# Reciprocal roots of the norms: one GpSimd power against eight VectorE steps

## The chip, the cores and the metric

The kernel runs on one core of a Trainium2 chip. The metric is the device time of one execution in microseconds (us), the median of several runs. A core has a matmul engine (PE, with its weight loads shown apart as PEld), a vector engine (DVE), a scalar engine (ACT), GpSimd (POOL) and a sync engine (SP) that issues most transfers. Each engine takes its instructions in the order in which the program lists them for that engine, and waits at an instruction whose inputs are not there yet.

## The reference

Two layers of a decoder trunk run for 256 prompt tokens and 8 sample tokens. Every norm is a root-mean-square norm:

```python
def rmsnorm(x, g):
    xf = x.astype(jnp.float32)
    y = xf * lax.rsqrt(jnp.mean(xf * xf, axis=-1, keepdims=True) + RMS_EPS)
    return (y * g.astype(jnp.float32)).astype(x.dtype)

yp = yp + 0.5 * swiglu(rmsnorm(yp, norm_ffn1[l]), ...)
h = rmsnorm(yp, norm_mix[l])                 # mixer: short convolution beside attention
q = (rmsnorm(q_c, q_a_norm) @ w_q_b)         # low-rank queries
ckv = rmsnorm(kv_c, kv_a_norm)               # low-rank keys and values
merged = concat([rmsnorm(conv_y, gn_conv), rmsnorm(attn_o, gn_attn)])
yp = yp + merged @ w_o
yp = yp + 0.5 * swiglu(rmsnorm(yp, norm_ffn2[l]), ...)
y = rmsnorm(yp, final_norm)                  # at the end
```

## The kernel before

**Layout.** Features lie on the 128 partitions and the 264 tokens (256 and 8) along the free axis. Weights come in chunks of up to 1 MB through three `raw` buffers. A unit of weights is split into a rounded half `hi` (ACT, L230) and a remainder `lo` (DVE, L232), two instructions of each kind per unit; a product is three matmuls, hi by hi, hi by lo, lo by hi (`mm3`, L249 to L251). Five `hi` and five `lo` buffers let units be split ahead of their use. When both units of a chunk are split, the next chunk is loaded.

**A norm.** The squares of a token are summed over the tiles into `ssA` or `ssB`. `sums` reduces 32 x 32 blocks on DVE (L310) and folds them with a small matmul (L311), so that each token's mean stands in one of nine block columns, a tile of 128 x 9. A small DVE instruction adds the epsilon (L345, L562, L909, L933), `rsqrt_of` raises the tile to the power -0.5 on GpSimd (L303), and `over_rows` turns the result into a row that every partition holds (L315). There are thirteen calls of `rsqrt_of`: six from `norm_stats` (each FFN and each mixer), two from `low_rank` (18 columns, keys and queries together), two each from `a_stats` and `c_stats`, and one of 3 columns at the end.

**Order.** The program is traced in an order written by hand (`ORDER` for the mixer; `H1`, `H2`, `N1`, `N2` for the places among the matmuls at which `norm_stats` and `norm_spread` are traced), and a planner then lists each engine's instructions. `behind()` adds an edge: the `lo` instructions that are traced after `after[0]` was set stand behind that instruction on DVE. Buffers of one tag are handed out in the order of tracing: `t264` has nine, `w` has four in the mixer.

**In the mixer** `low_rank` finds the roots for keys and queries, and `latent` spreads those of the keys (`Rk`, a `t264` tile, L315), makes the normalised keys `ckvf` (L570), and takes the query factors (L575, L580). `store_kpe` has matmuls that read `ckvf` (L746), `values` follows (L598 to L600). At the end of the mixer `a_stats` and `c_stats` lead to `a_spread` (L938, L939, `Ra`, L315, L944), whose output the last matmuls of the output projection need.

The tiles that the change touches:

```python
Rk = t264()
over_rows(Rk, s2[:, 0:NBLK])
V.tensor_tensor(ckvf, kvg, Rk[:, :T], ALU.mult)
...
Ra = t264()
over_rows(Ra, fa)
```

Of the kernel before, what the change touches and what calls it, by code (L numbers as in the profile page):

```python
# [7 lines left out]
F32 = mybir.dt.float32  # L8
F32R = mybir.dt.float32r
BF16 = mybir.dt.bfloat16  # L10
I32 = mybir.dt.int32
AF = mybir.ActivationFunctionType
ALU = mybir.AluOpType
AX = mybir.AxisListType
PSUM = bass.MemoryType.PSUM

P = 128
# [3 lines left out]
T = SEQ + NB  # L21

NBLK = -(-T // 32)
TP = 32 * NBLK
# [83 lines left out]
def trunk_kernel(ctx: ExitStack, tc: tile.TileContext, a: dict, o: dict):  # L108
    nc = tc.nc
    V, S, G, PE = nc.vector, nc.scalar, nc.gpsimd, nc.tensor  # L110

    cst = ctx.enter_context(tc.tile_pool(name="cst", bufs=1))
    stat = ctx.enter_context(tc.tile_pool(name="stat", bufs=1))
    tiny = ctx.enter_context(tc.tile_pool(name="tiny", bufs=3))
    tmp = ctx.enter_context(tc.tile_pool(name="tmp", bufs=TMP))
# [9 lines left out]
    def nm(s):  # L125
        n_of[0] += 1
        return f"{s}_{n_of[0]}"

    def t264(dt=F32):
        return tmp.tile([P, TP], dt, tag="t264", name=nm("t264"))  # L130

    def bank(tag):
        if tag == "mm":
            return pmm.tile([P, 512], F32, tag="mm", name=nm("mm"))
        return (paux if tag == "s" else pax3).tile([P, 512], F32, tag=tag, name=nm(tag))

    def small(w, dt=F32, tag=None):
        return tiny.tile([P, w], dt, tag=tag or f"sm{w}", name=nm("sm"))
# [8 lines left out]
    after = [None]  # L147

    def behind():

        return tc.issue_after(after[0]) if after[0] else nullcontext()
# [19 lines left out]
    for l in range(DEPTH):  # L171
# [4 lines left out]
        for c in (0, 2):  # L176
            for part in (1, 2, 0):
                f = part * CD + c * P
# [60 lines left out]
    def take():  # L239
        i = state["next"]  # L240
        state["next"] += 1
        return halves[i]
# [23 lines left out]
    nc.sync.dma_start(con, a["con"])  # L266
    load_chunk()
    tri = t264()[:, 0:P]
    nc.gpsimd.dma_start(tri, a["mask"])

# [11 lines left out]
    def gain(name, n, i=0):  # L282
        return gains[:, gat[name] + n + i:gat[name] + n + i + 1]
# [9 lines left out]
    spre = cst.tile([P, DEPTH, CT, NB], F32, name="spre")  # L293


    mhalf = cst.tile([P, 1], F32, name="mhalf")
    G.memset(mhalf, -0.5)
    fold = cst.tile([P, P], F32, name="fold")
    G.tensor_copy(fold.rearrange("p (a b) -> p a b", a=4), con[:, None, C_SUM:C_SUM + 32].to_broadcast([P, 4, 32]))

    def rsqrt_of(v, w):
        r = small(w, tag=f"rsr{w}")
        G.tensor_tensor(r, v, mhalf.to_broadcast([P, w]), ALU.pow)  # L303
        return r

    def sums(ps, ss, c0=0):


        q = small(NBLK, tag="sums")
        after[0] = V.tensor_reduce(q, ss.rearrange("p (c j) -> p c j", j=32), AX.X, ALU.add, apply_transpose=True).ins  # L310
        PE.matmul(ps[:, c0:c0 + NBLK], fold, q, start=True, stop=True)  # L311

    def over_rows(out, r):

        return V.transpose(out, r[:, :, None].to_broadcast([P, NBLK, 32]))  # L315
# [7 lines left out]
    def finish_y(kt, g, split=True, square=True, pool=False, last=False):  # L323
        if split:
            S.activation(xg["h"][:, kt], y[:, kt], AF.Copy, scale=g)  # L325
            V.scalar_tensor_tensor(xg["l"][:, kt], y[:, kt], g, xg["h"][:, kt].bitcast(F32), ALU.mult, ALU.subtract)  # L326
        if not square:
            return
        if kt == 0:
            S.activation(ssA[:, :T], y[:, kt], AF.Square, scale=D ** -0.5)  # L330
        else:
            sq = t264()
            S.activation(sq[:, :T], y[:, kt], AF.Square, scale=D ** -0.5)
            if kt == KT - 1 and last:
                nrm["sq"] = sq
                return
            (G if pool else V).tensor_tensor(ssA[:, :T], ssA[:, :T], sq[:, :T], ALU.add)
# [3 lines left out]
    def norm_stats():  # L341
        ps = bank("x")
        sums(ps, ssA)
        v = small(NBLK, tag="vn")
        V.tensor_scalar(v, ps[:, 0:NBLK], EPS, None, ALU.add)  # L345
        nrm["v"] = v
        nrm["r"] = rsqrt_of(v, NBLK)
# [23 lines left out]
    def ffn(next_gain, final=False, side=None, first=False):  # L371
# [12 lines left out]
        def evac_g(m, ps):  # L384
            g1 = t264()[:, :T]
            V.tensor_tensor(g1, ps[:, :T], Rb, ALU.mult)  # L386
            done()
            th = t264()[:, :T]
            S.activation(th, g1, AF.Tanh, scale=0.5)  # L389
            a1[m] = t264()[:, :T]  # L390
            evac[0] = V.scalar_tensor_tensor(a1[m], th, 1.0, g1, ALU.add, ALU.mult).ins  # L391
# [96 lines left out]
    def mixer(l):  # L488
# [3 lines left out]
        def mt(shape, tag, dt=F32, bufs=None):  # L492
            return mp.tile(shape, dt, tag=tag, name=nm(tag), **({"bufs": bufs} if bufs else {}))

        def r264():
            return mt([P, T], "r264", F32R, 8)

        def wtile(n=384):
            return mt([P, 384], "w", bufs=4)[:, 0:n]
# [57 lines left out]
        def low_rank():  # L557
            ps = bank("x")
            sums(ps, ssB)
            sums(ps, ssA, NBLK)  # L560
            v2 = small(2 * NBLK, tag="v2")
            V.tensor_tensor(v2.rearrange("p (n c) -> p n c", n=2), ps[:, 0:2 * NBLK].rearrange("p (n c) -> p n c", n=2),  # L562
                            ev[:, None, :].to_broadcast([P, 2, NBLK]), ALU.add)
            st["s2"] = rsqrt_of(v2, 2 * NBLK)

        def latent():
            s2 = st["s2"]
            Rk = t264()
            over_rows(Rk, s2[:, 0:NBLK])
            V.tensor_tensor(ckvf, kvg, Rk[:, :T], ALU.mult)  # L570
            ckh, ckl = r264(), r264()
            S.activation(ckh, ckvf, AF.Copy)

            sel = small(8, tag="qsel")
            V.scalar_tensor_tensor(sel.rearrange("p (c b) -> p c b", b=4), s2[:, NBLK:NBLK + 8].rearrange("p (c b) -> p c b", b=4),  # L575
                                   SCALE, con[:, None, C_BLK:C_BLK + 4].to_broadcast([P, 2, 4]), ALU.mult, ALU.mult)
            qsc = small(2, tag="qsc")
            V.tensor_reduce(qsc, sel.rearrange("p (c b) -> p c b", b=4), AX.X, ALU.add)
            sq8 = small(32, tag="sq8")
            after[0] = V.transpose(sq8, s2[:, 2 * NBLK - 1:2 * NBLK].to_broadcast([P, 32])).ins  # L580
            st["qsc"], st["sq8"] = qsc, sq8[:, 0:NB]
            V.tensor_tensor(ckl, ckvf, ckh.bitcast(F32), ALU.subtract)
            st["ckh"], st["ckl"] = ckh, ckl

            kp2 = t264()
            with behind():
                V.stream_shuffle(kp2[64:96, :T], kp1[64:96, :T], SWAP)
            V.tensor_tensor(kp1[64:96, :T], kp1[64:96, :T], cos[64:96], ALU.mult)
            V.tensor_tensor(kp2[64:96, :T], kp2[64:96, :T], sin[64:96], ALU.mult)
            V.tensor_tensor(kpf[64:96], kp1[64:96, :T], kp2[64:96, :T], ALU.add)  # L590
# [108 lines left out]
        def prompt():  # L699
            low_rank()  # L700
            yield
            latent()
            done(2)
            yield
# [199 lines left out]
        def c_stats():  # L904

            ps = bank("x")
            sums(ps, ssB)
            vc = small(NBLK, tag="vc")
            V.tensor_tensor(vc, ps[:, 0:NBLK], ev, ALU.add)  # L909
            st["sc"] = rsqrt_of(vc, NBLK)  # L910
            st["vc"] = vc
# [24 lines left out]
        def a_spread():  # L936
            fa = small(NBLK, tag="fa")
            V.tensor_tensor(fa, st["sa"], st["sc"], ALU.mult)  # L938
            V.tensor_tensor(fa, fa, st["vc"], ALU.mult)  # L939
            Ra = t264()  # L940
            over_rows(Ra, fa)
            for t in range(CT):
                f = t264()[:, :T]
                V.scalar_tensor_tensor(f, st["attn"][:, t], gain("gn_attn", 4 * l, t), Ra[:, :T], ALU.mult, ALU.mult)  # L944
                S.activation(mg[0][:, t], f, AF.Copy)
                V.tensor_tensor(mg[1][:, t], f, mg[0][:, t].bitcast(F32), ALU.subtract)
# [17 lines left out]
        for k in range(KT):  # L964
            for w, ps in zip(us, pss):
                o_part(ps, w, k)
            if k == 2:
                a_spread()
            if k == 5:
                c_spread()  # L970
            if k == 5:
                c_store()
        for m in range(4):
            o_finish(m, pss[m])
        for m in range(4, KT):
            w, ps = take(), bank("mm")
# [81 lines left out]
    v = small(3, tag="vn")  # L1058
# [11 lines left out]
    r = rsqrt_of(v, 3)  # L1070
# [66 lines left out]
```

## Time and profile before

| what | value |
|---|---|
| median of 3 runs | 1051.21 us (1051.0 to 1051.54) |
| the profiled execution, its own time | 1041.29 us |
| its span, first to last instruction | 1039.5 us |
| mean granted TensorE clock | 0.987 |
| busy: PE, DVE, ACT, POOL | 97%, 72%, 52%, 11% of the span |
| the thirteen powers on POOL | 28.0 us together |

Shares of busy time are means over stages with different limits. A wait row says which engine and line sat idle, what released it, the total, the count and the longest.

### The profile page before, as it was taken

To read this page: it belongs to the slowest core of one execution; us is meant where nothing else is said; L and a number is where in the kernel's file an instruction comes from. 1 tells how busy PE (TensorE), PEld (TensorE's weight loads), DVE (VectorE), ACT (ScalarE), POOL (GpSimd) and SP (SyncE) were. 2 spreads that over 40 slices of the span, in tenths; PEclk is the share of its full clock that TensorE was granted. 3 is DMA by queue.
4 is the path that set the end of the run, shared out by engine and by line. 5 is a ranking of instruction groups with operands and counts; after the bars stand their busy time and mean duration, and the time that the engine had idled before them with its cause. 6 is when DMAs were issued, how large, how long until landed. Compare 5 with 4: busy or idle time off the path is not lost.

```text
span 1039.5 us, 21546 instructions
## 1 busy us (share of the span) xinstructions
PE 1006.8 (97%) x8660; PEld 976.3 (94%) x8660; DVE 751.0 (72%) x1656; ACT 538.0 (52%) x1165; POOL 112.9 (11%) x140
## 2 busy tenths in 40 slices
PE   7999999989999999999999999999899999999996
PEld 6999999979788999999999999999778899999996
DVE  7888876669758877756678888566886887777551
ACT  6555545448535655545455555454675555555441
POOL 2111100040322000000011111001322210000000
PEclk9999999989999999999999999999899999999998
DMA  9767755545615655645557676554553356554531
GB/s 300 232 221 234 234 183 193 164 143 159 258 46 162 211 196 167 198 146 193 190 187 254 210 233 222 164 179 151 161 208 142 108 191 215 169 196 157 179 112 43
DMA packets 170772, 189.98 MB, mean 183 GB/s; under 512 B 3936, under 2 KB 163712, under 8 KB 170672
## 3 DMA queue, kind: packets, MB, share of 16 engines
q1 hardware_dynamic: 164048, 167.53, 50.0%
q0 software_dynamic: 5760, 19.42, 5.2%
q10 hardware_dynamic: 864, 1.64, 0.5%
q8 instruction: 68, 1.11, 0.5%
q14 instruction: 32, 0.26, 0.1%
HBM read 187.12 MB, written 1.49 MB: 181 GB/s over the span
## 4 chain that ended last, share of the span: by engine, by line
PE 70%; issue 20%; DVE 7%; ACT 1%; DMA 1%; POOL 1%; POOLq 0%; ACTq 0%; SPq 0%
PE mm L249 22%; PE mm L251 21%; PE mm L250 21%; DVE lo L232 2%; PE x L780 1%; PE s L650 1%; DVE y L955 1%; DVE xg L326 1%; PE x L819 1%; DMA raw<-in_w_ffn_gate_dram 1%; POOL sm L303 1%; PE x L687 1%; ACT hi L230 1%; PE x L674 1%; DVE t L954 1%
## 5 line engine op out<-in xcount | busy, mean ns | idle before, releaser
L230 ACT ACTIVATE hi<-raw 128x512 fp32r<-128x512 f32 (+1 forms) x648 | 365.4, 612 | 357.0 <-PE mm L250 236.2
L232 DVE TENSOR_TENSOR lo<-raw,hi 128x512 fp32r<-128x512 f32 (+1 forms) x648 | 414.6, 673 | 114.1 <-ACT hi L230 103.9
L249 PE MATMUL mm<-xg,hi 128*128 128x264 f32 x1648 | 472.0, 287 | 8.2 <-DVE t L954 3.1
L251 PE MATMUL mm<-xg,lo 128*128 128x264 f32 x1648 | 468.5, 285 | 0.9 <-DVE lo L232 0.9
L250 PE MATMUL mm<-xg,hi 128*128 128x264 f32 x1648 | 468.5, 284 | 0.0
L249 PEld LDWEIGHTS mm<-xg,hi 128*128 128x128 f32 x1648 | 311.8, 189 | 11.7 <-ACT hi L230 7.1
L251 PEld LDWEIGHTS mm<-xg,lo 128*128 128x128 f32 x1648 | 310.2, 188 | 3.1 <-DVE lo L232 1.8
L250 PEld LDWEIGHTS mm<-xg,hi 128*128 128x128 f32 x1648 | 311.9, 189 | 0.8 <-issue 0.8
L249 PE MATMUL mm<-act,hi 128*128 128x264 f32 x704 | 200.4, 285 | 0.0
L251 PE MATMUL mm<-act,lo 128*128 128x264 f32 x704 | 199.7, 284 | 0.0
L250 PE MATMUL mm<-act,hi 128*128 128x264 f32 x704 | 199.2, 283 | 0.0
L249 PEld LDWEIGHTS mm<-act,hi 128*128 128x128 f32 x704 | 132.3, 188 | 0.2 <-ACT t L1025 0.2
L251 PEld LDWEIGHTS mm<-act,lo 128*128 128x128 f32 x704 | 132.5, 188 | 0.0
L250 PEld LDWEIGHTS mm<-act,hi 128*128 128x128 f32 x704 | 132.4, 188 | 0.0
L456 POOL DMA_INDIRECT nat<-in_cache_ckv_dram,idx x32 | 31.9, 996 | 420.3 <-DVE B L480 187.3
L386 DVE TENSOR_TENSOR t<-mm,Rw 128x264 f32<-128x264 f32 x88 | 37.8, 429 | 43.1 <-PE mm L251 42.8
L395 DVE TENSOR_TENSOR t<-mm,t 128x264 f32<-128x264 f32 x88 | 37.5, 428 | 40.9 <-PE mm L251 40.3
L303 POOL TENSOR_TENSOR sm<-sm,mhalf 128x9 f32<-128x9 f32 (+2 forms) x13 | 28.0, 2155 | 244.6 <-DVE sm L1069 190.4
L325 ACT ACTIVATE xg<-y,gains 128x264 fp32r<-128x264 f32 x48 | 24.1, 513 | 30.0 <-DVE y L441 19.1
L398 DVE TENSOR_TENSOR act<-t,act 128x264 fp32r<-128x264 f32 x88 | 37.7, 429 | 0.9 <-ACT act L397 0.8
L391 DVE SCALAR_TENSOR_TENSOR t<-t,t 128x264 f32<-128x264 f32 x88 | 37.7, 428 | 0.2 <-ACT t L389 0.2
L389 ACT ACTIVATE t<-t 128x264 f32<-128x264 f32 x88 | 36.1, 411 | 2.1 <-DVE t L386 2.1
(219 smaller groups left out, 837.2 us busy)
## 6 DMA issues: line engine op xcount, KB each, us to landing
raw<-in_w_ffn_up_dram SPq DMA_DIRECT2D x44, 1024.0 KB, 5.2
raw<-in_w_ffn_gate_dram SPq DMA_DIRECT2D x43, 1024.0 KB, 5.2
raw<-in_w_ffn_down_dram SPq DMA_DIRECT2D x32, 1024.0 KB, 5.4
raw<-in_w_in_dram SPq DMA_DIRECT2D x14, 1024.0 KB, 5.3
raw<-in_w_ffn_down_dram SPq DMA_DIRECT2D x16, 768.0 KB, 4.6
raw<-in_w_o_dram SPq DMA_DIRECT2D x8, 1024.0 KB, 5.4
raw<-in_w_q_dram SPq DMA_DIRECT2D x2, 768.0 KB, 4.3
raw<-in_w_in_dram SPq DMA_DIRECT2D x2, 640.0 KB, 4.3
```

The source lines that it names most:

```text
L230: S.activation(h[:, k, f], raw[:, k, lo:hi][:, :, f], AF.Copy)
L232: V.tensor_tensor(r[:, k, f], raw[:, k, lo:hi][:, :, f], h[:, k, f].bitcast(F32), ALU.subtract)
L249: PE.matmul(ps, wh, xh, start=start, stop=False)
L250: PE.matmul(ps, wh, xl, start=False, stop=False)
L251: return PE.matmul(ps, wl, xh, start=False, stop=stop)
L303: G.tensor_tensor(r, v, mhalf.to_broadcast([P, w]), ALU.pow)
L386: V.tensor_tensor(g1, ps[:, :T], Rb, ALU.mult)
L389: S.activation(th, g1, AF.Tanh, scale=0.5)
L391: evac[0] = V.scalar_tensor_tensor(a1[m], th, 1.0, g1, ALU.add, ALU.mult).ins
L395: V.tensor_tensor(t, ps[:, :T], a1.pop(m), ALU.mult)
L398: evac[0] = V.tensor_tensor(al[:, m], t, ah[:, m].bitcast(F32), ALU.subtract).ins
L456: G.indirect_dma_start(dst, None, src, bass.IndirectOffsetOnAxis(ap=idx[l][:, b:b + 1], axis=0))
```

## The change

`rsqrt_of` no longer uses GpSimd. It takes a first guess from the bits of the number, as an integer (-0.5 times the bits plus a constant), and improves it in two rounds: three instructions and then four, each reading the one before it. That makes eight DVE instructions on the small tile. `after[0]`, behind which later `lo` instructions stand, is now the last of these eight steps and no longer the block reduce in `sums`. `Rk` and `Ra` come from the tag `w` instead of `t264`, whose tiles shrink from 288 to 266 columns, and the constant `mhalf` is gone.

```diff
     def t264(dt=F32):
-        return tmp.tile([P, TP], dt, tag="t264", name=nm("t264"))
+        return tmp.tile([P, T + 2], dt, tag="t264", name=nm("t264"))
...
-    mhalf = cst.tile([P, 1], F32, name="mhalf")
-    G.memset(mhalf, -0.5)
...
     def rsqrt_of(v, w):
+
         r = small(w, tag=f"rsr{w}")
-        G.tensor_tensor(r, v, mhalf.to_broadcast([P, w]), ALU.pow)
+        t = small(w, tag=f"rst{w}")
+        V.tensor_scalar(r.bitcast(I32), v.bitcast(I32), -0.5, float(0x5F3759DF), ALU.mult, ALU.add)
+        V.scalar_tensor_tensor(t, r, -0.1875, r, ALU.mult, ALU.mult)
+        V.tensor_tensor(t, t, v, ALU.mult)
+        V.scalar_tensor_tensor(r, t, 0.5625, r, ALU.add, ALU.mult)
+        V.scalar_tensor_tensor(t, r, -64.0 / 9.0, r, ALU.mult, ALU.mult)
+        V.tensor_tensor(t, t, v, ALU.mult)
+        V.scalar_tensor_tensor(t, t, 10.0 / 3.0, t, ALU.add, ALU.mult)
+        after[0] = V.scalar_tensor_tensor(r, t, 5.0, r, ALU.add, ALU.mult).ins
         return r
...
-        after[0] = V.tensor_reduce(q, ss.rearrange("p (c j) -> p c j", j=32), AX.X, ALU.add, apply_transpose=True).ins
+        V.tensor_reduce(q, ss.rearrange("p (c j) -> p c j", j=32), AX.X, ALU.add, apply_transpose=True)
...
             s2 = st["s2"]
-            Rk = t264()
+            Rk = wtile(TP)
             over_rows(Rk, s2[:, 0:NBLK])
...
-            Ra = t264()
+            Ra = wtile(TP)
             over_rows(Ra, fa)
```

## Rows read from the trace of the kernel before

**Rows 1.** The page, busy time: us, share of the span, instructions.

```profile
PE 1006.8 (97%) x8660; PEld 976.3 (94%) x8660; DVE 751.0 (72%) x1656; ACT 538.0 (52%) x1165; POOL 112.9 (11%) x140
```

**Rows 2.** Waits of PE: line and releaser, total us, times, longest.

```profile
PE x L746 <- issue: 9.1, 2, 4.6
PE mm L249 <- DVE t L954: 3.1, 2, 1.5
PE mm L249 <- ACT qg L945: 3.0, 2, 1.5
...
PE mm L249 <- DVE t L386: 1.9, 1, 1.9
```

**Rows 3.** The powers (L303): shortest, median, longest in ns, then forms.

```profile
L303 POOL TENSOR_TENSOR sm<-sm,mhalf x13: 850/2126/3592, 20.7 to 1031.7; 128x9 f32<-128x9 f32 x10, 128x18 f32<-128x18 f32 x2, 128x3 f32<-128x3 f32 x1
```

**Rows 4.** DVE in order of time in the first mixer: start, us, instruction, idle before.

```profile
219.80 0.47 DVE L310 TRANSPOSE_TENSOR_REDUCE sm<-ssA 128x9 f32<-128x288 f32 x1
220.19 0.65 DVE L232 TENSOR_TENSOR lo<-raw,hi 128x512 fp32r<-128x512 f32 x1
...
221.10 0.17 DVE L562 TENSOR_TENSOR sm<-x,sm 128x18 f32<-128x18 f32 x1
221.19 0.68 DVE L232 TENSOR_TENSOR lo<-raw,hi 128x512 fp32r<-128x512 f32 x1
224.97 0.17 DVE L575 SCALAR_TENSOR_TENSOR sm<-sm,con 128x8 f32<-128x8 f32 x1 [3.10 <-POOL sm L303]
...
226.63 0.42 DVE L871 TENSOR_TENSOR t<-mm,R 128x264 f32<-128x264 f32 x1
226.97 0.46 DVE L315 STREAM_TRANSPOSE t<-sm 128x288 f32<-128x288 f32 x1
...
227.94 0.43 DVE L570 TENSOR_TENSOR ckvf<-t,t 128x264 f32<-128x264 f32 x1
```

**Rows 5.** PE in order of time, where it starts again in the first mixer.

```profile
228.48 1.08 PE L746 MATMUL x<-con,ckvf 128*32 128x128 f32 x16 [4.58 <-issue]
```

**Rows 6.** Stretches: length, busy us of each engine, granted clock, DMA share, GB/s.

```profile
26.50:29.50 3.00, 3.00 (x15) 3.00 (x15) 2.30 (x11) 1.17 (x3) 0.83 (x1) 0.50 0.69 206
223.90:228.50 4.60, 0.02 (x4) 0.05 (x5) 3.43 (x12) 1.46 (x4) 1.04 (x1) 0.91 0.59 204
228.50:234.50 6.00, 6.00 (x33) 5.05 (x34) 4.68 (x9) 2.88 (x7) 5.25 (x13) 0.50 0.60 184
225.00:245.00 20.00, 16.52 (x120) 15.60 (x121) 17.75 (x44) 11.20 (x27) 5.60 (x16) 0.83 0.45 143
245.00:260.00 15.00, 14.22 (x113) 13.45 (x112) 14.43 (x45) 12.70 (x35) 0.53 (x1) 1.00 0.59 184
```

**Rows 7.** DVE in order of time, two small instructions, the second reading the first.

```profile
211.09 0.17 DVE L345 TENSOR_SCALAR sm<-x 128x9 f32<-128x9 f32 x1 [0.20 <-PE x L311]
211.29 0.17 DVE L521 TENSOR_SCALAR sm<-sm 128x9 f32<-128x9 f32 x1
```

**Rows 8.** DVE in order of time at the first FFN.

```profile
20.34 0.17 DVE L345 TENSOR_SCALAR sm<-x 128x9 f32<-128x9 f32 x1 [0.74 <-PE x L311]
20.42 1.89 DVE L232 TENSOR_TENSOR lo<-raw,hi 128x512 fp32r<-128x512 f32 x3
...
23.21 0.46 DVE L315 STREAM_TRANSPOSE Rw<-sm 128x288 f32<-128x288 f32 x1
...
24.18 0.41 DVE L386 TENSOR_TENSOR t<-mm,Rw 128x264 f32<-128x264 f32 x1
```

**Rows 9.** DVE in order of time at the end of the first mixer.

```profile
302.07 0.16 DVE L909 TENSOR_TENSOR sm<-x,sm 128x9 f32<-128x9 f32 x1
...
304.50 0.17 DVE L938 TENSOR_TENSOR sm<-sm,sm 128x9 f32<-128x9 f32 x1 [1.68 <-POOL sm L303]
```

**Rows 10.** The last norm, all engines in order of time.

```profile
1031.43 0.14 DVE L1069 TENSOR_TENSOR sm<-sm,mm 64x1 f32<-64x1 f32 x1
...
1032.53 0.75 DVE L1076 TENSOR_SCALAR fin<-x,sm 128x512 f32<-128x512 f32 x1 [0.96 <-POOL sm L303]
```

## The prediction

> **What bounds the kernel now.** The page comes first: PE is busy 97% of the span, DVE 72%, POOL 11% [rows 1]. So a faster root is worth something only where PE stands still for it, or where DVE is the engine that PE waits for. The waits of PE say where that is [rows 2]. The longest stand at L746, 9.1 us in two waits, one in each mixer. The profile puts them to "issue", but L746 reads `ckvf`: PE starts at 228.48 [rows 5], and L570, which makes `ckvf`, ends at 227.94 + 0.43 = 228.37 [rows 4]. So these are waits for the norm of the keys. There are 3.0 us at the last step of the output projection (ACT L945, behind `a_spread`) and 1.9 us once at L386, behind the first FFN's root. The 3.1 us at L954 belong to the residual sums after the output projection, which the change doesn't touch. No wait of PE belongs to the five other calls in `norm_stats`: their powers stand under the matmuls of the first units.
>
> Then DVE in order of time [rows 4]: it sits idle for 3.10 us in front of L575 until the power is there. After that it takes another 3.4 us to the end of L570, because the splits of later weights, L871 and a shuffle stand between. L315 follows right on L871. `Rk` is the `t264` tile handed out after that of L871, so I read this as the order of the buffers and not as a want of time.
>
> Last the stretches [rows 6]: PE does nothing from 223.9 to 228.5, and from 228.5 to 234.5 its granted clock is 0.50, the lower of its two levels (1.2 of 2.4 GHz). The same follows the 1.9 us at the first FFN: 0.50 from 26.5 to 29.5. DVE is busy 17.75 of 20 us from 225 to 245 and 14.43 of 15 from 245 to 260, with PE busy throughout or nearly so. The two engines are close to balance there, and this decides how much of a gain in front is kept.
>
> **The price of the steps.** The trace has no such chain, but it has two small DVE instructions of which the second reads the first: they start 0.20 us apart and last 0.17 [rows 7]. Eight steps, each reading the one before, take 8 x 0.20 = 1.6 us, and with the 0.2 from the start of the instruction ahead to the first step, 1.8 us from that start to the first reader. Where neighbours don't depend on each other they start 0.09 apart (221.10 and 221.19) [rows 4], so other work can be slipped between the steps, and the bounds of what DVE loses are 8 x 0.09 = 0.7 and 1.6 us a call. I take 1.6, since the splits near at hand are held behind the last step (below). The eighteen columns of `low_rank` change little, as L562 with 18 columns takes 0.17 as well [rows 4].
>
> The Trainium skill, VectorE: DVE Perf Modes, section "The DRAIN you can't avoid", speaks against the change: a next operation doesn't start until the pipe is empty, so one should keep the number of operations small. Its formula for a two-input operation, (N + 151)/0.96, gives 167 ns for nine columns, so by the page eight steps would take 1.34 us, an estimate, lost to all other work. The trace agrees on the length of one; it doesn't agree that neighbours never overlap.
>
> **Removed and added, call by call.**
>
> *low_rank, twice.* The power takes 3.59 us with 18 columns [rows 3]. From the start of L562 to L575 it is 224.97 - 221.10 = 3.87 us now and would be 1.8: the roots come 2.07 us earlier, at 222.9. Two `lo` splits ran ahead of the power, at 220.19 and 221.19, right behind the reduce of 219.80 [rows 4]. They are traced after `low_rank`, so the new edge holds them until the last step. They cost DVE some 0.6 us each, so its lead is 2.07 - 1.2 = 0.87 us. `Rk` no longer waits its turn behind L871: L315 and L570 (0.46 and 0.43) can follow at once, which puts `ckvf` at 223.8, or at 225.0 if the two splits go first. PE ran out of work at 223.9, so its wait falls from 4.6 to between nothing and 1.2 us.
>
> What is late next? PE would have 4.0 us of the wait back (the middle) and, if its clock stays up, half of the 6.0 us at 0.50: 7.0 us a mixer. DVE can't follow so far: it has its lead of 0.87 and idle time of 2.25 and 0.57 us up to 260 to fill [rows 6]. So a mixer gains between 0.9 us (DVE keeps its pauses) and 3.7 us (it fills all). The largest part of the pauses lies where PE ran at half clock, which speaks for the upper half; that the chain from 245 on is nearly all DVE speaks against all of it. I take 2.4: 4.8 us for both.
>
> *a_stats and c_stats, twice.* From L909 to L938 it is 2.43 us [rows 9] and would be 1.8: 0.6 us of the 1.5 that PE waits each time [rows 2]. The eight steps of `a_stats` may push back the last squares ahead of L909 by as much. Bounds 0 and 0.6; I take 0.3: 0.6 us for both.
>
> *The first FFN.* From L345 to L315 it is 23.21 - 20.34 = 2.87 us [rows 8] and would be 1.8 if L315 goes next: 1.07 us earlier, and if that keeps the clock up, half of the 3.0 us at 0.50 comes back too: 2.6 us at best. Against it, the three splits of 20.42 (1.89 us [rows 8]) and one more behind the reduce are held until the last step. If they then go ahead of L315, it comes at 22.14 + 2.5 = 24.6, 1.4 us later than now. Middle: a gain of 0.6 us.
>
> *The end.* From L1069 to L1076 it is 1.10 us [rows 10], since the power of three columns takes only 0.85 [rows 3]. Eight steps make it 1.5 to 1.8: a loss of 0.4 to 0.7, nothing hides it. I take 0.5.
>
> *The five other calls* cost nothing, because the matmuls of the first units cover them; without that cover each would gain the 2.13 us of the median power [rows 3] less the 1.6 of the steps, 0.5 us. The narrower `t264` tiles and the new place of `Ra` I put at nothing: the row operations keep their lengths, and four `w` buffers are free by then.
>
> Sum: 4.8 + 0.6 + 0.6 - 0.5 = 5.5 us less. The profiled execution took 1041.29 us with a span of 1039.5, so by itself it would come to 1035.8. The median of the runs is 1051.2, some 10 us above that execution. I take the difference over as it stands: 1051.2 - 5.5 = 1045.7 us.
>
> **The rivals.**
>
> *PE gets all of it.* If the splits between 225 and 260 are not what PE waits for, each mixer gives the 7.0 us of PE: 14.0 + 0.6 + 0.6 - 0.5 = 14.7 us, 1036.5. For it: PE is shown busy through all of 228.5 to 234.5, at half clock. Against it: the pauses of DVE hold only 2.8 us up to 260.
>
> *Nothing is left.* DVE is the bound from the stall on and keeps its pauses, 0.9 us a mixer, the first FFN gives nothing, and the end costs 0.5: 1.3 us less, 1049.9. For it: the chain through DVE from 245 on. Against it: the pauses at half clock have their cause taken away.
>
> *Held splits make it slower.* The edge to the last step piles the splits up behind the roots, and the planner may list more of them ahead of L315 and L570 than now. The point from which it decides is `ckvf` at 228.4: from 222.9 there is room for 5.5 us, of which L315 and L570 take 0.9, so 4.6 us of other work. Now 2.5 us stand between [rows 4], and the two held splits make it 3.7. Two more splits, those of the next chunk, make 4.9: each mixer then loses 0.3 us, the first FFN 1.4 and the end 0.5, together 2.5: 1053.7. For it: DVE's list is in order and the edge is new at all calls. Against it: `Rk` isn't tied to L871 any more, and it is traced before the splits of the next chunk.
>
> **How the numbers follow.** 0.2% of the time is 2.1 us, about what a measurement of this kernel can tell from no change. The forecast, a gain of 2.1 to 11 us, has a chance of 0.62; PE gets all 0.10; nothing is left 0.16; slower 0.12. So faster 0.72, the same 0.16, slower 0.12. The upper bounds of all calls together give 7.4 + 1.2 + 2.6 - 0.4 = 10.8 us, 1040.4; the lower ones 1.8 + 0 - 1.4 - 0.7, a loss of 0.3, 1051.5. I widen the low end to 1039.5 for part of the first rival and leave the rest of it and the slower case outside.
>
> **What would show it.** Right: eight DVE instructions of some 0.16 us at 0.20 from each other at each of thirteen calls, no work of POOL at L303; L575 about 1.8 us after L562; L315 and L570 soon after it and no longer tied to L871; the wait at L746 below 1.5 us and a granted clock of 1.00 behind it; about 1.6 us from L1069 to L1076. Wrong: L746 still waiting over 3 us, steps that lie further apart than 0.2 us, a wait of PE for `lo` that wasn't there, or a DVE list from 225 to 260 in another order whose pauses are as long as now.

## The result and the profile after

The changed kernel takes 1041.13 us (median of 4 runs, 1040.1 to 1042.19) against 1051.38 us (4 runs, 1051.0 to 1051.79): ratio 0.990, 95% interval 0.9887 to 0.9912, so 10.2 us less. The forecast was 1045.7 us, range 1039.5 to 1051.5, and faster. The direction and the shorter wait for the keys' norm came as forecast. That the time lies inside the range is luck: the sum stands on a profile that lacks the place where most of the rest was gained, as the repeated run of before shows below.

The page of the changed kernel, busy time:

```profile
PE 1006.1 (97%) x8660; PEld 973.6 (94%) x8660; DVE 765.1 (74%) x1760; ACT 538.3 (52%) x1165; POOL 84.9 (8%) x126
```

POOL lost the 28.0 us of powers and DVE got 104 instructions (1760 - 1656), thirteen times eight [rows 1]. DVE in order of time in the first mixer, beside [rows 4]:

```profile
219.69 0.17 DVE L569 TENSOR_TENSOR sm<-x,sm 128x18 f32<-128x18 f32 x1
219.89 0.18 DVE L303 TENSOR_SCALAR sm<-sm 128x18 int32<-128x18 int32 x1
...
221.38 0.18 DVE L310 SCALAR_TENSOR_TENSOR sm<-sm,sm 128x18 f32<-128x18 f32 x1
221.47 1.29 DVE L232 TENSOR_TENSOR lo<-raw,hi 128x512 fp32r<-128x512 f32 x2
222.69 0.43 DVE L878 TENSOR_TENSOR t<-mm,R 128x264 f32<-128x264 f32 x1
223.03 0.47 DVE L322 STREAM_TRANSPOSE w<-sm 128x288 f32<-128x288 f32 x1
...
223.60 0.39 DVE L577 TENSOR_TENSOR ckvf<-t,w 128x264 f32<-128x264 f32 x1
```

The eight steps start 0.21 us apart, and the roots are there 1.78 us (219.69 to 221.47) after the start of the instruction ahead of them, where the power took 3.87. Two `lo` splits and the multiplication by `R` (now L878) still stand ahead of the spread of the keys' root (now L322).

The waits of PE, beside [rows 2] (L746 is now L753, L674 is L681, L801 is L808, L945 is L952; lines of `rsqrt_of` are L303 to L310):

```profile
PE mm L249 <- ACT hi L230: 4.4, 2, 3.1
PE mm L249 <- ACT qg L952: 3.7, 2, 1.8
PE mm L249 <- DVE t L961: 3.1, 2, 1.5
PE x L753 <- issue: 2.9, 2, 1.4
PE x L681 <- DVE w L674: 2.5, 3, 1.6
PE x L681 <- DVE lo L232: 1.6, 1, 1.6
...
PE x L808 <- issue: 1.1, 2, 0.6
```

The wait for the normalised keys fell from 9.1 to 2.9 us. The first row holds the first matmul's wait for its weights and the wait of 1.35 us in the first FFN (1.9 before). The wait ahead of the output projection rose from 3.0 to 3.7, and the waits at L681 rose from 0.7 (L674 in before) to 4.1, for `lo` splits and for attention weights, both made by DVE. A wait of PE for `lo` where there was none is one of the prediction's own signs of being wrong.

Stretches of the changed kernel (length, busy us of each engine, granted clock, DMA share, GB/s): behind the restart in the first mixer, the same in the second, and from the first restart to the first transpose of L835. Then before from its restart to the same transpose, L828 there:

```profile
224.10:229.40 5.30, 4.84 (x31) 3.96 (x32) 5.08 (x11) 2.50 (x6) 4.88 (x12) 0.68 0.65 218
730.00:735.30 5.30, 4.83 (x40) 3.87 (x41) 5.08 (x11) 3.04 (x8) 4.67 (x13) 1.00 0.66 216
224.09:286.54 62.45, 58.54 (x685) 48.42 (x686) 51.66 (x157) 39.84 (x109) 15.27 (x29) 0.97 0.61 206
```

```profile
228.48:287.50 59.02, 58.06 (x683) 48.88 (x683) 50.35 (x153) 39.68 (x109) 15.55 (x29) 0.95 0.58 200
```

For the same matmuls PE needs 62.45 us where it needed 59.02. It stands still for 3.9 us of it (62.45 - 58.54) instead of 1.0. DVE is busy for 51.66 us instead of 50.35, with four instructions more behind the restart: three `lo` splits of 0.55 us and the multiplication of L588, which in before started while PE stood at L746 (225.19 to 226.16, and 228.41). The planner also lists PE's work in another order here: 18 more of the long matmuls stand ahead of the short ones of L808 than stood ahead of L801. That the moved DVE work causes the new waits is read from what ended them (L681 waits for DVE); no run isolates it.

### The profile page after: what moved, and what is told of

Its sections match the earlier page's. It is cut to its first block, busy times and chain, and to the rows that moved or that the text cites. A ratio compares the mean times of both kernels' runs of the same rounds, so it can differ in the third digit from the quotient of the medians.

```text
span 1038.8 us, 21642 instructions
## 1 busy us (share of the span) xinstructions
PE 1006.1 (97%) x8660; PEld 973.6 (94%) x8660; DVE 765.1 (74%) x1760; ACT 538.3 (52%) x1165; POOL 84.9 (8%) x126
## 3 DMA queue, kind: packets, MB, share of 16 engines
q8 instruction: 68, 1.11, 0.4%
## 4 chain that ended last, share of the span: by engine, by line
PE 65%; DVE 9%; ACT 2%; issue 1%; ACTq 0%
PE mm L249 20%; PE mm L251 20%; PE mm L250 20%; DVE lo L232 3%; PE s L657 1%; PE x L787 1%; DVE y L962 1%; PE x L826 1%; PE x L681 1%; DVE xg L333 1%; PE x L694 1%; DVE t L961 1%; PE s L658 0%; ACT hi L230 0%; DVE qg L645 0%
## 5 line engine op out<-in xcount | busy, mean ns | idle before, releaser
L404 ACT ACTIVATE act<-t 128x264 fp32r<-128x264 f32 x88 | 35.7, 410 | 1.6 <-DVE t L402 1.1
```

What stands on the lines that cost most here:

```text
L404: S.activation(ah[:, m], t, AF.Copy)
```

## The experiments

Each run's time is a median, beside before on the same chip, with the 95% interval of the ratio.

**Which before is the usual one.** The profiled execution took 1041.29 us, the median 1051.21. The kernel before was run once more, unchanged.

> The kernel before, unchanged. Its profiled execution had a span of 1039.5 us beside a median time of 1051.2 us, while the changed kernel has spans of 1037.6 to 1039.7 us beside 1041.1. Theory: that profiled execution was an uncommon one, and in most executions the core itself takes longer: spans near 1048.7 us (the time less 2.5), with a mean granted clock lower than 0.987. Rival: the core's work is as long as in that profile and the 10 us lie outside of the span: spans near 1039.5 us at a clock of 0.987, with times of 1051.

Measured: 1051.91 us (11 runs) against 1052.25 (15 runs), ratio 0.9994 [0.9985, 1.0003], and this time a profile with a span of 1047.8, so the 10 us lie inside the span, as the theory said; the mean granted clock of that execution was 0.987, not lower than in the first profile. It took 1049.58 us, one of the two quickest of the eleven, so some 2 us of the median are not in this profile. PE in order of time at L801, the last of POOL's gathers of cached rows (L456), and PE at the same place in the first profile:

```profile
271.60 0.47 PE L801 MATMUL x<-con,ws 128*32 128x32 f32 x33
272.51 0.23 PE L801 MATMUL x<-con,ws 128*32 128x32 f32 x2 [0.44 <-issue]
273.96 0.21 PE L801 MATMUL x<-con,ws 128*32 128x32 f32 x1 [1.22 <-issue]
274.68 0.21 PE L801 MATMUL x<-con,ws 128*32 128x32 f32 x1 [0.51 <-issue]
275.39 0.64 PE L801 MATMUL x<-con,ws 128*32 128x32 f32 x27 [0.50 <-issue]
```

```profile
272.12 0.94 POOL L456 DMA_INDIRECT nat<-in_cache_ckv_dram,idx  x1 [0.30 <-issue]
273.36 0.94 POOL L456 DMA_INDIRECT nat<-in_cache_ckv_dram,idx  x1 [0.30 <-issue]
```

```profile
272.42 0.76 PE L801 MATMUL x<-con,ws 128*32 128x32 f32 x64
```

In the run of 64 short matmuls PE is stopped, with a few matmuls between, for 3.3 us (272.07 to 275.39). Its granted clock is 0.50 from 273.23 on, and behind the stop:

```profile
275.40:280.00 4.60, 4.60 (x43) 4.11 (x44) 1.48 (x4) 1.31 (x4) 0.00 (x0) 0.50 0.63 249
```

The same comes in the second mixer (781.72 to 785.03). In the profile that the prediction stood on, all 64 pass in 0.76 us. Cutting the span at the same six instructions shows what this means (us; the cuts are the first matmul of each mixer, the restart behind the keys' norm, the first transpose of L828, now L835):

| stretch | before, first profile | before, repeated | after |
|---|---|---|---|
| start to first mixer | 206.41 | 205.42 | 205.15 |
| to the restart at `ckvf` | 22.07 | 22.05 | 18.94 |
| to the transpose | 59.02 | 64.41 | 62.45 |
| to the second mixer | 424.22 | 423.82 | 424.48 |
| to the restart at `ckvf` | 22.06 | 22.06 | 18.92 |
| to the transpose | 59.00 | 63.29 | 61.64 |
| to the end | 246.71 | 246.77 | 247.21 |
| span | 1039.49 | 1047.82 | 1038.79 |

Against the repeated profile the change gains 3.1 us in front of each restart and 2.0 and 1.6 behind it. Against the first profile the same 3.1 us are given back behind it (3.4 and 2.6), and the whole span differs by 0.7 us. On which chip the first profile was taken isn't on record. One more difference lies outside the span: a run's time less its span is 2.5 us in the changed kernel (2.46 to 2.50 in its four runs) and 1.8 in before (1.72 to 1.84). So the change loses 0.7 us there; the forecast had no such term, and its cause is open.

**The tag alone.** Before, with `Rk` and `Ra` from `w`, and the powers kept.

```diff
-            Rk = t264()
+            Rk = wtile(TP)
...
-            Ra = t264()
+            Ra = wtile(TP)
```

> The kernel before with one part of the change: Rk and Ra come from the tag w, the roots stay powers on GpSimd. Theory (the wait for the keys' norm sets the gain, and half of its shortening comes from Rk no longer standing behind L871): L315 of Rk starts within 0.5 us after L575's neighbours, ckvf is there some 2.0 us earlier than at 228.4, the wait at L746 falls from 4.6 to about 2.6 us, and the time from 1051.3 to about 1047. Rival (only the power itself matters): the wait stays above 4 us and the time within 1050 to 1052.

Measured: 1043.67 us (1041.69 to 1044.08) against 1052.25, ratio 0.9914 [0.9901, 0.9928]. DVE in order of time:

```profile
223.60 0.48 DVE L315 STREAM_TRANSPOSE w<-sm 128x288 f32<-128x288 f32 x1 [3.10 <-POOL sm L303]
...
225.40 0.42 DVE L871 TENSOR_TENSOR t<-mm,R 128x264 f32<-128x264 f32 x1
```

L315 now runs the moment the power is done and L871 comes later: it was the order of the buffers that held it. The wait at L746 falls from 4.6 to 2.1 us with the slow power still in place, which the theory had (2.6); the time is 3 us below its 1047, and the stop at L801 falls to 0.5 us too.

**The power back in `low_rank` alone.** The changed kernel, except that the calls with 18 columns use the GpSimd power.

> The changed kernel with the power on GpSimd in low_rank alone (two of thirteen calls), the eight steps in the other eleven. Theory (nearly all of the gain comes from the two low_rank calls): the wait at L753 (L746 before) is 2 us or more longer than the 1.44 of the changed kernel, and at least half of the 10.2 us is lost again, 1046 us or more. Rival (the gain comes from the first FFN, the ends of the mixers or the smaller places): within 2 us of 1041.1.

Measured: 1044.98 us (1042.07 to 1046.55), ratio 0.9922 [0.9909, 0.9936]. The wait for the keys is 2.2 us. Both theories missed: the wait is 0.8 us longer than 1.44 and not 2, and the time is 3.9 us above 1041.1 and not within 2. Like the tag alone, this version keeps most of the gain.

**The steps alone.** Before, with the eight steps and the new edge, but `Rk` and `Ra` in `t264` (the scratch tiles of the steps are shared so that all fits).

> The eight steps and the splits' edge alone: Rk and Ra come from t264 again (the scratch tiles of the steps are made smaller so that it fits). Theory (either part by itself shortens the wait for the keys' norm enough to leave the bad place at L801): the roots come 2 us earlier, Rk still stands behind L871, the wait at the first matmul that reads ckvf is 1.4 to 3 us, and the time is 1041 to 1046. Rival (only the place of Rk matters, the steps give nothing): the wait is above 4 us and the time 1050 or more.

Measured: 1041.29 us (1039.69 to 1042.56) against 1051.23, ratio 0.990 [0.9884, 0.9917], wait for the keys 1.44 us. So the steps by themselves bring all of it, and the tag alone most of it: with either of them the stop at L801 is short (0.5 us), and the two don't add up. With the steps, DVE's order in front of the restart is the same with `t264` as with `w`: two splits, the multiplication by `R`, the spread. Behind the same wait of 1.44 us the granted clock stays at 1.00 here:

```profile
223.00:228.30 5.30, 4.85 (x40) 3.87 (x41) 5.08 (x11) 3.28 (x9) 4.88 (x12) 1.00 0.66 219
```

The changed kernel once more, on the same chip:

> The changed kernel again, beside the other three on one chip. All theories: 1040 to 1042 us, spans 2.5 us less, the wait at L753 about 1.4 us in each mixer and at most 0.6 us of stops inside the run at L808.

Measured: 1041.4 us (1040.59 to 1042.29), ratio 0.9903 [0.9887, 0.9918].

**The edge.** The changed kernel with `after[0]` set at the block reduce again.

```diff
-        after[0] = V.scalar_tensor_tensor(r, t, 5.0, r, ALU.add, ALU.mult).ins
+        V.scalar_tensor_tensor(r, t, 5.0, r, ALU.add, ALU.mult)
...
-        V.tensor_reduce(q, ss.rearrange("p (c j) -> p c j", j=32), AX.X, ALU.add, apply_transpose=True)
+        after[0] = V.tensor_reduce(q, ss.rearrange("p (c j) -> p c j", j=32), AX.X, ALU.add, apply_transpose=True).ins
```

> The changed kernel with the splits' edge put back: after[0] is the block reduce again and not the last step. Theory (the edge costs little at the roots and only shifts splits): two splits run beside the steps again, the wait at L753 is between 0.2 and 1.5 us, and the time within 2 us of 1041.1. Rival (the edge is what keeps the steps together, and without it the planner slips splits of 0.6 us between the steps): the eight steps of low_rank take over 2.5 us, the wait at L753 is over 2 us, and the time is 1044 or more.

Measured: 1043.56 us (1042.62 to 1043.87), ratio 0.9915 [0.9901, 0.9928]. DVE in the first FFN:

```profile
21.98 0.17 DVE L303 TENSOR_SCALAR sm<-sm 128x9 int32<-128x9 int32 x1
22.05 0.68 DVE L232 TENSOR_TENSOR lo<-raw,hi 128x512 fp32r<-128x512 f32 x1
22.65 0.16 DVE L304 SCALAR_TENSOR_TENSOR sm<-sm 128x9 f32<-128x9 f32 x1
...
26.27 0.16 DVE L310 SCALAR_TENSOR_TENSOR sm<-sm,sm 128x9 f32<-128x9 f32 x1
```

Splits slip in between the steps, which take 4.3 us from the first to the last (21.98 to 26.27) instead of 1.4, and PE waits 3.8 us there instead of 1.35. In the mixer the other order is better: the wait for the keys is 0.9 us, since one of the two held splits now runs ahead of the steps.

**Is it the traffic of the gathers that stops PE?** In the repeated profile the late gathers filled the transfer engines at L801 (DMA share 1.02 from 270 to 278 us). Both kernels were run with those gathers cut to a quarter of their bytes (they fetch other rows, and the matmuls read them again in place of the rest); the order on PE, DVE and ACT is unchanged.

```diff
-                gather(nat[:, b].rearrange("p t c -> p (t c)"), "cache_ckv", l, 4 * s + b)
+                gather(nat[:, b, 0:2].rearrange("p t c -> p (t c)"), "cache_ckv", l, 4 * s + b, 2)
...
-                    PE.matmul(po[32 * b:32 * b + 8, 0:P], PT[:, t, 8 * b:8 * b + 8], nat[:, b, t], start=False,
+                    PE.matmul(po[32 * b:32 * b + 8, 0:P], PT[:, t, 8 * b:8 * b + 8], nat[:, b, t % 2], start=False,
```

> The kernel before, with the eight late gathers of each mixer (L784, the rows of the cache for the sample output) fetching 128 x 256 instead of 128 x 1024; it reads other rows and only a quarter of the bytes, and the order on PE, DVE and ACT stays the same. Theory: in the kernel before PE stops inside its run of 64 small matmuls at L801 because its next block of instructions waits behind these gathers, and the half clock that follows costs as much again. Without the traffic the stops at L801 (3.2 us in the first mixer of the second profile) go, no half clock follows there, and the time falls from 1052 to 1043 to 1046 us. Rival (the stops have another cause, such as ACT or DVE being late): the stops stay and the time is within 2 us of 1052.

> The changed kernel with the same small gathers (other rows, a quarter of the bytes). Theory: the changed kernel has lost only some 0.5 us a mixer to waits for instructions at this place, so it gains little, to 1039 to 1041.5 us, and the distance to the kernel before with the same gathers shrinks from 10 to 1 to 5 us: the rest of the 10 us was the missing stop and its half clock. Rival (the gathers cost both kernels alike): both fall by the same amount and the distance stays 9 to 10 us.

Measured: before with a quarter 1051.83 us, ratio 1.0004 [0.9992, 1.0015], with a DMA share of 0.25 from 270 to 278; after with a quarter 1040.65, ratio 0.9896 [0.9879, 0.9913]. PE at L801 in the former:

```profile
272.22 0.46 PE L801 MATMUL x<-con,ws 128*32 128x32 f32 x32
...
275.94 0.65 PE L801 MATMUL x<-con,ws 128*32 128x32 f32 x28 [0.53 <-issue]
```

The stop is as long as ever (272.68 to 275.94). The theory of the traffic fell.

**Is it a place in PE's list?** The stops came at nearly the same count of matmuls in every trace so far, the 2139th to 2145th in the first mixer, so forty matmuls of one column were put at the very start of both kernels; the other four engines' lists stay as they are.

```diff
-    for _ in range(WARM):
-        PE.matmul(ps[:, 0:2 * P], wz[:, 0:P], wz, start=True, stop=True)
+    for i in range(WARM + 40):
+        PE.matmul(ps[:, 0:(2 * P if i < WARM else 1)], wz[:, 0:P], wz[:, 0:(2 * P if i < WARM else 1)], start=True, stop=True)
```

> The kernel before with forty more matmuls of one column each at the very start, behind the warm-up ones, and nothing else. It asks whether the stop of PE in the run of matmuls at L801 (3.3 us in both mixers of the two repeated runs of before, followed by a granted clock of 0.50) goes with a place in PE's list of instructions or with a place in time. Theory of the place in the list: the stop comes forty matmuls earlier in the program, ahead of L801 or at its first matmuls, and the time moves only by what the stop costs there: 1044 to 1053 us. Rival, the place in time or in the computation: the stop stays within the same matmuls of L801, wait at L746 stays 4.6 us, 1050 to 1053 us.

> The changed kernel with the same forty one-column matmuls at the start. Theory of the place in the list: the short stops of 0.5 us at L808 come forty matmuls earlier, the time stays within 1040 to 1043 us if they stay short and goes to 1044 to 1047 us if one becomes as long as in the kernel before. Rival: they stay at L808, 1040 to 1043 us. In both, the wait for the normalised keys stays 1.4 us.

Measured: before shifted 1051.46 us, ratio 1.0007 [0.9993, 1.0021]; after shifted 1040.53, ratio 0.990 [0.988, 0.992]. In the former the stop is in the same matmuls of L801 (271.41 to 274.64), forty further on in the list. The place in the list fell too. In the latter the short stops at L808 are gone, which neither text had, and the time is much the same. Nor is it the loading of PE's program, which the theory of the traffic supposed: in the shifted before no transfer of instructions is under way in either stop (the nearest end at 269.52 and begin at 277.82 us, and end at 781.69 and begin at 788.97).

These runs together show a regularity. Long or short, each of the nineteen stops at this line, in ten traces, ends 0.94 to 1.11 us after the last of POOL's eight late gathers has ended: 275.39 behind 274.30 (273.36 + 0.94) above; in the changed kernel 271.87 behind 270.78:

```profile
270.90 0.43 PE L808 MATMUL x<-con,ws 128*32 128x32 f32 x18
271.87 0.71 PE L808 MATMUL x<-con,ws 128*32 128x32 f32 x46 [0.53 <-issue]
```

```profile
269.84 0.94 POOL L463 DMA_INDIRECT nat<-in_cache_ckv_dram,idx  x1 [0.30 <-issue]
```

Where the last gather had ended 1.6 us or more ahead of the first short matmul, there is no stop (both mixers with the edge put back and with the list shifted, the second mixer of the repeated changed kernel). The change fits: the first gather starts behind the scores of L780 (now L787), 3.5 us earlier (263.45 to 259.99), and the last one ends 3.5 us earlier (274.30 to 270.78), while L808 comes only 0.7 us earlier (271.60 to 270.90), behind 18 more long matmuls and PE's new waits. So the gathers are over when PE comes to the short matmuls.

**Taking half of the late gathers away** was to test this. Before, with the second group of sequences reading the cached rows of the first; the lists of PE, DVE, ACT and SP are unchanged.

```diff
-            nat = keep.tile([P, 4, NSLOT, KV], F32, tag="B", bufs=2, name=nm("nat"))
-            for b in range(4):
+            nat = st["nat", 0] if s else keep.tile([P, 4, NSLOT, KV], F32, tag="B", bufs=2, name=nm("nat"))
+            for b in range(0 if s else 4):
```

> The kernel before with four of the eight late gathers of each mixer left out: the second group of sequences reads the cached rows of the first group (so its samples get other rows), and the order of the instructions on PE, DVE, ACT and SP is unchanged. In every run that had the 3.3 us stop of PE at L801, the second four gathers of GpSimd (L456, 0.94 us each, 1.25 us apart) were still running at that place, and the stop ended 1.0 to 1.1 us after the last of them; in the changed kernel they were done before PE came to these matmuls. Theory: the gathers hold PE up there; with only the first four, which end some 3 us before L801, no stop of more than 0.2 us, no granted clock of 0.50 behind it, 5.4 and 4.3 us less from the restart at L746 to the transposes at L815 in the two mixers, the 4.6 us wait at L746 unchanged, so 1040 to 1044 us. Rival: the run of sixty-four short matmuls stops by itself or for another reason: stop of 3 us in both mixers, 1049 to 1053 us.

Measured: 1039.97 us (11 runs, 1038.66 to 1041.15), just under what the theory said, and no stop: all 64 pass in 0.76 us (271.60 to 272.36).

But the unchanged kernel before, on the same chip, took 1040.64 us (15 runs, 1039.12 to 1041.69): ratio 0.9994 [0.9985, 1.0003]. This series was on another chip than those before it, and there before is as quick as in the prediction's profile (1041.29). So the run proves nothing on the gathers. It does show that the 10 us are not there in every series: before takes 1051 to 1052 us in the four others, on two chips as far as they are on record, and 1041 in this one, on a third. That it is the chip and not something else of the series is likely and not shown. The changed kernel was not run there, so what the change is worth on that chip is open.

**A version that is faster than both.** The changed kernel with two edits from the runs above: for `low_rank` the edge goes back to the reduce, and the root of three columns at the end is the power again.

```diff
+        if w == 3:
+            G.tensor_tensor(r, v, mhalf.to_broadcast([P, w]), ALU.pow)
+            return r
...
+        last = V.scalar_tensor_tensor(r, t, 5.0, r, ALU.add, ALU.mult).ins
+        if w != 2 * NBLK:
+            after[0] = last
...
+        if ss is ssB or c0:
+            after[0] = red
```

> The changed kernel with two edits that the runs so far suggest: for the calls of low_rank alone the edge for later lo splits goes back to the block reduce (the wait for the normalised keys was 0.9 us with that edge and 1.4 without), and the root of three columns at the end is the GpSimd power again (0.85 us against eight steps). Theory: the wait for the normalised keys 0.9 to 1.0 us in both mixers, the wait at the first FFN stays 1.35 us, the last stage 0.2 to 0.6 us shorter; 1039.0 to 1041.0 us. Rival: VectorE is the bound behind the wait, so what is gained in front is given back before the output projection: 1041.0 to 1042.5 us, no difference from the changed kernel.

Measured: 1038.84 us (1037.45 to 1039.21), ratio 0.9879 [0.9857, 0.9902]; the shifted changed kernel on the same chip took 1040.53 (1040.14 to 1042.21), so some 1.7 us less. Of these 1.0 lies inside the span (medians 1037.1 and 1038.05) and 0.7 outside, where this version has before's 1.8 us again. Stretch behind the restart, and the end on DVE (lines nine further on than in the changed kernel):

```profile
223.50:229.00 5.50, 5.42 (x45) 4.46 (x46) 5.32 (x14) 3.81 (x10) 4.69 (x13) 1.00 0.40 140
```

```profile
1029.46 0.14 DVE L1085 TENSOR_TENSOR sm<-sm,mm 64x1 f32<-64x1 f32 x1
1030.61 0.75 DVE L1092 TENSOR_SCALAR fin<-x,sm 128x512 f32<-128x512 f32 x1 [1.01 <-POOL sm L305]
```

The waits for the keys' norm are 0.91 us where they were 1.44, and the end is 0.6 us shorter (1.15 from L1085 to L1092). The clock of 1.00 is no gain over the shifted changed kernel, whose clock stayed at 1.00 behind its 1.44 us as well.

## Why the prediction was right, and where it was not

**The price of the steps** held: 0.20 apart with nine columns, 0.21 with eighteen, 1.78 us in all where 1.8 was forecast. The formula of the Trainium skill that was weighed (VectorE: DVE Perf Modes; it stands in the section "The TRN2 errata", where it is checked at 512 and 2048 columns) gave an estimate of 167 ns for one step; the trace shows 0.17. By the estimate of 1.34 us for eight the steps would be quicker than they are: steps that read each other start 0.20 us apart. In the section "The DRAIN you can't avoid" of that page a next operation waits for the pipe to empty, but the section adds that one that is not held starts earlier, which the prediction left out. The trace agrees with the addition: the first `lo` split starts 0.09 us after the last step (221.38, 221.47).

***low_rank*, in front**: the mechanism right, the wait 0.2 us over the bound. The two held splits went first, and PE waits 1.44 us, forecast nothing to 1.2. `ckvf` was done at 223.99 and not at 225.0, but that is because the whole mixer starts 1.26 us earlier (205.15 and 206.41 in the table): counted from there it is 18.84 us where 18.6 was forecast. The step that `Rk` no longer waits its turn behind L871 did not come true: L878 still stands ahead of the spread, and with `Rk` in `t264` the wait is the same 1.44. The tag helps where the power is kept. And the clock of 1.00 that was expected behind the wait is not sure to come: in this profile it came in the second mixer and not in the first, and of the ten waits of 1.44 us in five profiles of the changed kernel and its near variants, two were followed by a fall to 0.50.

***low_rank*, behind**: this term was mis-sized, and with it the base that it was added to. The step was: a mixer gains between 0.9 and 3.7 us, "I take 2.4", on the profile's own span. On that span it came to -0.3 and +0.5 us (3.1 in front, 3.4 and 2.6 given back), below the lower bound. The argument that "DVE can't follow so far" was right and taken too weakly: the stall had been time in which DVE worked ahead, and four of its instructions now come behind the restart, where PE stands still for 2.9 us more, the most of it at L681 for DVE. On that profile "nothing is left" was the nearer rival (1.3 us against 0.7 in the span). The first profile and the changed kernel may come from different chips, so these two differences are no measurement on one chip.

**The base** failed: "I take the difference over as it stands". The 10 us between the profiled execution and the median were not a fixed amount on top of the kernel. By the table the repeated profile loses 5.4 and 4.3 us in the two stretches that hold L801 (the other rows take 1.4 off), and there the change wins 2.0 and 1.6 us. So against the repeated profile the stretches in front of and behind the two restarts give 3.1 + 2.0 and 3.1 + 1.6, together 9.9 us, of which the other stretches give 0.8 back (the spans differ by 9.0). The forecast of 5.5 us is neither this nor the 0.7 of the first profile.

**The first FFN**: a gain of 0.6 was forecast. From the start of L352 (21.16) to the spread it is 2.33 us where it was 2.87, and the wait fell by as much, from 1.9 to 1.35 us. One of the held splits stands ahead of the spread:

```profile
22.80 0.17 DVE L310 SCALAR_TENSOR_TENSOR sm<-sm,sm 128x9 f32<-128x9 f32 x1
22.89 0.69 DVE L232 TENSOR_TENSOR lo<-raw,hi 128x512 fp32r<-128x512 f32 x1
23.49 0.47 DVE L322 STREAM_TRANSPOSE Rw<-sm 128x288 f32<-128x288 f32 x1
```

Up to the first mixer 0.3 us are left of it against the repeated profile and 1.3 against the first. The difference goes with the clock: the fall to 0.50 from 26.5 to 29.5, of which the forecast put half into its upper bound, comes in the first profile only. In the five other profiles of before and its variants with this wait of 1.89 us the clock stays up.

***a_stats* and *c_stats***: a gain of 0.3 each was forecast; it became a loss of 0.3 each (1.84 against 1.52 in the first mixer). The steps are quicker than the power (1.72 us from L916 to the first instruction behind them, against 2.43 from L909 to L938 [rows 9]), but two `lo` splits stand behind them, at 302.76 and 303.88, where in before two ran ahead of the power's end:

```profile
301.04 0.17 DVE L916 TENSOR_TENSOR sm<-x,sm 128x9 f32<-128x9 f32 x1 [0.23 <-PE x L318]
...
302.76 0.69 DVE L232 TENSOR_TENSOR lo<-raw,hi 128x512 fp32r<-128x512 f32 x1
303.36 0.16 DVE L945 TENSOR_TENSOR sm<-sm,sm 128x9 f32<-128x9 f32 x1
...
303.88 0.68 DVE L232 TENSOR_TENSOR lo<-raw,hi 128x512 fp32r<-128x512 f32 x1
304.48 0.47 DVE L322 STREAM_TRANSPOSE w<-sm 128x288 f32<-128x288 f32 x1
```

From L916 to the `qg` of ACT it is 4.47 us (301.04 to 305.51) where it was 4.12 (302.07 to 306.19).

**The end**: a loss of 0.4 to 0.7 was forecast; from L1076 (1030.57) to L1083 (1032.32) it is 1.75 us against 1.10 [rows 10], 0.65 us.

**Held splits** didn't make it slower, and the edge that this rival feared is what protects the first FFN: without it PE loses 2.5 us more there.

**What stays open.** Why PE stops at L801, and why before does so in most series and not in all. The amount of traffic, the place in the list and the loading of instructions are ruled out. That the gathers are the cause is a regularity of nineteen stops, not shown by an edit. Against it alone: in the first profile of before the gathers were running at L801 too (272.62 to 273.56 and 273.87 to 274.83), and PE passed. So it is not shown either that the changed kernel gains by ending its gathers earlier; shown is that its stop is short and that of before long.

## What to carry to other kernels

Before a sum is made against a profile, compare the profiled execution's own time with the median; if they differ by more than the change is worth, get a second profile and find the place of the difference, since the change may act just there. A stall of PE is not all loss when the engine that feeds it works ahead in that time: count what that engine did in the stall, because it will have to be done later. And an edge that keeps long work from slipping between short dependent steps should be set call by call: it is worth 2.5 us of PE's wait at the first FFN, and costs half a us where other work could have gone first. And a fall of the clock that one profile shows behind a short wait should not be counted as a gain before a second profile shows it too.

## What the runs showed of the hardware

- In a run of 64 short matmuls PE can stop with nothing that the profile shows to wait for: 3.3 us in the repeated profile, in pieces of 0.4 to 1.2 us (it starts again at 272.51, 273.96, 274.68, 275.39), with a granted clock of 0.50 from 273.2 to 280.1. It is the same line in both mixers, and in the first profile it isn't there (0.76 us for all 64).
- The same kernel has medians of 1051 to 1052 us in four series, on chips 14 and 15 where the chip is on record, and 1041 us in one on chip 3, with ranges that don't meet (1048.25 at the lowest, 1041.69 at the highest).
- Behind equal short waits of PE the granted clock sometimes falls to 0.50 and mostly doesn't. Of ten waits of 1.44 us for the keys' norm two were followed by a fall (both times in the first mixer, from 225.96 to 229.38 in the changed kernel and from 226.11 to 229.52 in its repetition); of six waits of 1.89 us in the first FFN one was (26.26 to 29.67 in the first profile). Behind the ten waits of 4.6 us and the four of 2.1 to 2.2 us it was 0.50 each time, and behind the four of 0.91 us never.
